# Sample units of an attention kernel: cached keys stored feature by key, their gain moved to the queries

## The chip, the cores and the metric

The kernel runs on one core of a Trainium2 chip, in one launch. The metric is the device time of one execution in microseconds (us).

## The reference

One inference step of a two-layer encoder on a prompt of 1024 tokens and on 8 running streams ("samples") of 16 tokens each, model width 1024, 16 query heads, 4 key/value heads, head width 64. Layer A attends over a window of its own chunk and two before, with a penalty on distance and a learned sink; layer B over its own chunk and eight before, with a learned bias. Both end in a squared-ReLU MLP. What matters here is the attention of the samples, over 128 cached positions and the 16 new ones:

```
k = rmsnorm(k, g_k); q = rmsnorm(q, g_q)          # new tokens
k_all = concatenate([cache_k, k], axis=1)          # 128 cached + 16 new
s = einsum('bqhgd,bkhd->bhgqk', q, k_all) * 64**-0.5 + bias
p = softmax(s)                                     # with a sink in layer A
o = einsum('bhgqk,bkhd->bqhgd', p, v_all)
```

The cached keys come normed and with g_k in them; g_q and the factor 1/8 belong to the queries.

## The kernel before

Tokens stand in nine tiles of 128: eight of the prompt and one, called ST, that holds the 8 x 16 sample tokens. Each layer has an attention stage (0 to about 425 us and 1110 to 1640 us of the trace) and an MLP stage (the rest). All products run on TensorE in fp32r, where a value is kept as a high and a low part (`split`, L127: ScalarE writes the high part, VectorE or GpSimd the difference), so that a projection takes three products per block.

In the attention stage a loop over 16 steps takes two groups (a prompt tile and a key/value head) per step through scores, softmax, transposes of the probabilities (`ps_tr`, L326) and the product with the values (`ps_pv`, L333 and L334). Projections of queries, keys and output (L219 to L221, L176 to L178) are woven in between. Beside them step s carries sample unit U(s): key/value head j = s // 4 and a pair bp = s % 4 of sample streams. A unit is a generator of five pieces that the loop inserts into two steps:

- piece 0 loads the cached keys `kc` and values `vc` of the two streams (128 keys by 2 x 64 features), the queries `qu` (high and low part stacked over 128 partitions, and once swapped), and the 32 new keys into the last 32 columns of `kb`; it multiplies `kc` by the gain g_q x (-1/8) (L560, on GpSimd in layer A, on VectorE in layer B, by the letter c of the layer's `eng`), and writes high and low part side by side into `uks` (L570, L571, both GpSimd);
- piece 1 multiplies each stream's `uks` (keys by [high, low]) with the identity on TensorE, which turns it into features by keys, the high part on partitions 0 to 63 and the low part on 64 to 127 (L577, two products per unit, into `ps_utr`), and ScalarE copies that into `kb` (L578);
- piece 2 makes the scores, two products of 288 columns (L582), and the softmax of the unit on VectorE and ScalarE; piece 3 transposes the probabilities (L607 to L609), piece 4 multiplies them with the values (L615 to L617) and stores the result.

`kc`, `uks` and `kb` have one buffer each. The gain stands on the keys everywhere: of the prompt's and of the new sample keys in `k_stack` (L302), where the new sample keys take only g_q (kout is given), since they have been multiplied by g_k for the output (L295). Queries are normed without a gain in `q_stage1` (L224 to L242), transposed in `q_stage2`, and those of ST go through DRAM to the units.

What the order of instructions is: the program text gives dependences and priorities, and the framework's scheduler then orders each engine's queue by a model of its own. An edit in one piece therefore moves rows on every engine in the same stage.

Of the kernel before, what the change touches and what calls it, by code (L numbers as in the profile page):

```python
# [8 lines left out]
F32 = mybir.dt.float32  # L9
F32R = mybir.dt.float32r  # L10
AF = mybir.ActivationFunctionType
ALU = mybir.AluOpType
# [4 lines left out]
P = 128  # L17
# [3 lines left out]
ST = NT  # L21
NTILE = NT + 1
H = 16
KV = 4
G = 4
HD = 64
# [68 lines left out]
class Build:  # L95
# [127 lines left out]
    def q_stage1(self, work, small, ps, t, nb, fold):  # L223
        nc = self.nc  # L224
        ps3 = ps.rearrange("p (h d) -> p h d", d=HD)
        qn = self.scratch([P, 8, HD], F32, "qn")
        qr = work.tile([P, 8, HD], F32, tag="qr", name="qr", bufs=self.qrb)
        nc.scalar.activation(qn, ps3, AF.Square)
        nc.scalar.copy(qr, ps3)
        ssq = small.tile([P, 8], F32, tag="qssq", name="qssq")  # L230
        nc.vector.tensor_reduce(ssq, qn, AX.X, ALU.add)
        ms = small.tile([P, 8], F32, tag="qms", name="qms")
        e = self.ex[:, t : t + 1]
        if fold:
            c = C_SL2 + nb * 8
            nc.vector.scalar_tensor_tensor(ms, ssq, e, self.cst[:, c : c + 8], ALU.add, ALU.mult)
        else:
            nc.vector.tensor_scalar(ms, ssq, e, 1.0 / HD, ALU.add, ALU.mult)
        rs = small.tile([P, 8], F32, tag="qrs", name="qrs")
        nc.gpsimd.tensor_tensor(rs, ms, self.mhalf[:, 0:8], ALU.pow)  # L240
        self.eng("q").tensor_tensor(qr, qr, rs.unsqueeze(2).to_broadcast([P, 8, HD]), ALU.mult)
        return qr  # L242

    def q_stage2(self, qpool, qr, t):
# [25 lines left out]
    def kv_stage1(self, work, small, ps, t, gk, gq8, gkq8, vst, v8, kout, vout):  # L270
        nc = self.nc
        ps3 = ps[:, 0:256].rearrange("p (h d) -> p h d", d=HD)
        kw = work.tile([P, 2, KV, HD], F32, tag="kw", name="kw")
        kr, kn = kw[:, 0], kw[:, 1]
        r = self.rx[:, t : t + 1]
        if vst is not None:
            pv3 = ps[:, 256:512].rearrange("p (h d) -> p h d", d=HD)
            nc.scalar.activation(vst[:, :, 0:HD], pv3, AF.Copy, scale=r)
            nc.vector.scalar_tensor_tensor(
                vst[:, :, HD:P], pv3, r, vst[:, :, 0:HD].bitcast(F32), ALU.mult, ALU.subtract  # L280
            )
        if vout is not None:
            vsb = v8 if v8 is not None else self.scratch([P, 256], F32, "vsb")
            nc.scalar.activation(vsb, ps[:, 256:512], AF.Copy, scale=r)
        nc.scalar.copy(kr, ps3)
        nc.scalar.activation(kn, ps3, AF.Square)
        ssq = small.tile([P, KV], F32, tag="kssq", name="kssq")
        nc.vector.tensor_reduce(ssq, kn, AX.X, ALU.add)
        ms = small.tile([P, KV], F32, tag="kms", name="kms")
        nc.vector.tensor_scalar(ms, ssq, self.ex[:, t : t + 1], 1.0 / HD, ALU.add, ALU.mult)  # L290
        rs = small.tile([P, KV], F32, tag="krs", name="krs")
        nc.gpsimd.tensor_tensor(rs, ms, self.mhalf[:, 0:KV], ALU.pow)
        nc.vector.tensor_tensor(kn, kr, rs.unsqueeze(2).to_broadcast([P, KV, HD]), ALU.mult)
        if kout is not None:
            nc.vector.tensor_tensor(kn, kn, gk.unsqueeze(1).to_broadcast([P, KV, HD]), ALU.mult)  # L295
            nc.sync.dma_start(kout, kn.rearrange("p h d -> p (h d)"))
        if vout is not None:
            nc.sync.dma_start(vout, vsb)
        return self.k_stack(work, kn, gq8 if kout is not None else gkq8)

    def k_stack(self, work, kn, gq8):
        nc = self.nc  # L302
        ks = work.tile([P, KV, HD], F32, tag="ks", name="ks")
        nc.vector.tensor_tensor(ks, kn, gq8.unsqueeze(1).to_broadcast([P, KV, HD]), ALU.mult)
        return ks

    def k_transpose(self, ks, dst):
# [228 lines left out]
                self.qT8d[layer][2 * nb + j], qTs[j].rearrange("p h q -> p (h q)").bitcast(F32)  # L536
            )

    def unit(self, up, small, layer, bp, j, v8, gq8, cache_k, cache_v):
        nc = self.nc  # L540
        kc = up.tile([P, 2, HD], F32, tag="kc", name="kc")
        nc.sync.dma_start(kc, cache_k[2 * bp : 2 * bp + 2, :, j, :].rearrange("b k d -> k b d"))
        vc = up.tile([P, 2, HD], F32, tag="vc", name="vc")
        nc.sync.dma_start(vc, cache_v[2 * bp : 2 * bp + 2, :, j, :].rearrange("b k d -> k b d"))
        qu = up.tile([P, 2, P], F32R, tag="qu", name="qu")
# [4 lines left out]
        kb = up.tile([P, 288], F32R, tag="kb", name="kb")  # L550
# [5 lines left out]
        else:  # L556
            bias = up.tile([P, 288], F32, tag="ub", name="ub")
            nc.sync.dma_start(bias, self.biasSd[j])
        kp = kc
        self.eng("c").tensor_tensor(kp, kc, gq8.unsqueeze(1).to_broadcast([P, 2, HD]), ALU.mult)  # L560
        if "p" in self.engs:
            yield
            a, b = slice(0, 64), slice(64, 128)
            pt = self.psum("u", [P, P], "ps_utr")
            nc.tensor.transpose(pt, kp.rearrange("p b d -> p (b d)"), self.ident)
            self.split(kb[a, 0:P], kb[b, 0:P], pt[a])
            self.split(kb[b, P : 2 * P], kb[a, P : 2 * P], pt[b])
        else:
            ks = up.tile([P, 2, P], F32R, tag="uks", name="uks")
            nc.gpsimd.tensor_copy(ks[:, :, 0:HD], kp)  # L570
            self.eng("u").tensor_tensor(  # L571
                ks[:, :, HD:P], kp, ks[:, :, 0:HD].bitcast(F32), ALU.subtract
            )
            yield
            pt = self.psum("u", [P, 2, P], "ps_utr")
            for b in range(2):
                nc.tensor.matmul(pt[:, b, :], ks[:, b, :], self.identr, start=True, stop=True)  # L577
            nc.scalar.copy(kb[:, 0:256], pt.rearrange("p b k -> p (b k)"))  # L578
        yield
        s = self.psum("u", [P, 288], "ps_us")  # L580
        for v in range(2):
# [4 lines left out]
        p = up.tile([P, 288], F32, tag="sp", name="sp") if layer == 0 else bias  # L586
# [782 lines left out]
    def attention(self, layer):  # L1369
        nc, I = self.nc, self.ins  # L1370
        A = layer == 0
        if A:
            wkv_src, kv0, gkv = I["w_qkv_a"][0], 1024, 0
            wq_src, gq = I["w_qkv_a"][0], 0
            wo_src = I["w_o_a"][0]
            g_k, g_q = I["g_k_a"][0], I["g_q_a"][0]
            ck, cv = I["cache_k_a"][0], I["cache_v_a"][0]
        else:
            wkv_src, kv0, gkv = I["w_kv"], 0, 4
            wq_src, gq = I["w_q_b"][0], 1  # L1380
            wo_src = I["w_o_b"][0]
            g_k, g_q = I["g_k_b"], I["g_q_b"][0]
            ck, cv = I["cache_k_b"], I["cache_v_b"]
        cfg = CFG[layer]
        psp = () if A else cfg["psp"]
        self.engs = cfg["eng"]
# [1 line left out]
        with ExitStack() as st:  # L1388
# [187 lines left out]

            def U(n):
                j, bp = n // 4, n % 4
                return self.unit(up, small, layer, bp, j, v8, gq8, ck, cv)

            def addend():
                self.last = self.scratch([P, 4, P], F32, "o2")
# [80 lines left out]
                if not cfg["late"]:  # L1663
                    N(ST, "p")
            gk = self.load_gvec(ring, g_k, "gk")
            gq8 = self.load_gvec(ring, g_q, "gq", -0.125)
            gkq8 = ring.tile([P, HD], F32, tag="gkq", name="gkq")
            nc.vector.tensor_tensor(gkq8, gk, gq8, ALU.mult)
            if A:
# [107 lines left out]
            for s in range(2 * NT):  # L1777
                u = U(s)
# [133 lines left out]
```

## Time and profile before

| | |
|---|---|
| median of 3 runs | 2356.03 us |
| the three runs | 2350.42, 2356.03, 2356.86 us |
| span of the profiled execution | 2349.6 us |
| time of the profiled execution outside its span | not recorded; its span lies 0.8 us under the fastest run |
| TensorE matmuls | busy 2273.2 us, 97% of the span |
| TensorE weight loads | busy 1899.3 us, 81% |
| VectorE, ScalarE, GpSimd | 73%, 57%, 27% |
| idle TensorE by the page | 2349.6 - 2273.2 = 76.4 us |

PE is TensorE's matmuls, PEld its weight loads, DVE VectorE, ACT ScalarE, POOL GpSimd, SP SyncE, which issues most transfers. A matmul's recorded duration overlaps those of its neighbours, since they are pipelined; what one occupies is read from the distance between starts. A wait names the line that waited and the line whose end released it. L12 is line 12 of the kernel before.

### The profile page before, as it was taken

The page shows a single profiled execution, that of the slowest core. Times are in us where ns is not written, and L with a number is a line of the kernel's source. Part 1 is how long each engine was busy: PE and PEld are TensorE (multiplying, and loading weights), DVE is VectorE, ACT ScalarE, POOL GpSimd, SP SyncE. Part 2 cuts the span into 40 slices and gives each one's busy share as a digit, 9 for nine tenths or more (in the row PEclk, how much of TensorE's full clock was granted, in tenths as well). Part 3 has the DMA queues.
Part 4 walks back from the last instruction along what each step waited for, and adds up shares of the span by engine and source line. Part 5 has one row for each costly group of instructions (what it writes and reads, how often), then busy time and mean ns, then how long its engine had stood idle before and what let it go on. Part 6 is the DMA issues. An engine that isn't in the chain of part 4 may idle for free.

```text
span 2349.6 us, 33397 instructions
## 1 busy us (share of the span) xinstructions
PE 2273.2 (97%) x11429; PEld 1899.3 (81%) x11429; DVE 1718.3 (73%) x3075; ACT 1332.0 (57%) x2684; POOL 644.7 (27%) x950
## 2 busy tenths in 40 slices
PE   8999999899999999999899899999899999999999
PEld 6787877788888888778778778887888888888887
DVE  6888786766656578898577776877666566678987
ACT  3777674555555555344377666665655555555443
POOL 4434332313213111002433444345132132210011
PEclk9999999999999999999999999999999999999999
DMA  7435546234334687848654656555243343877567
GB/s 262 128 103 177 166 141 208 89 122 162 132 112 152 218 231 174 272 142 206 191 157 114 190 151 180 166 172 186 72 162 132 114 160 113 276 212 197 183 165 198
DMA packets 226715, 392.70 MB, mean 167 GB/s; under 512 B 51592, under 2 KB 126288, under 8 KB 226448
## 3 DMA queue, kind: packets, MB, share of 16 engines
q1 hardware_dynamic: 188816, 283.58, 37.8%
q0 software_dynamic: 36432, 102.26, 16.0%
q10 hardware_dynamic: 1296, 4.72, 0.5%
q8 instruction: 90, 1.47, 0.3%
q14 instruction: 81, 0.66, 0.1%
HBM read 236.51 MB, written 156.85 MB: 167 GB/s over the span
## 4 chain that ended last, share of the span: by engine, by line
PE 73%; DVE 11%; DMA 8%; ACT 3%; issue 2%; POOL 2%; SPq 1%; ACTq 0%; DVEq 0%; POOLq 0%
PE ps_c L745 7%; PE ps_c L746 7%; PE ps_c L747 7%; PE ps_x L745 5%; PE ps_x L747 5%; PE ps_x L746 5%; PE ps_mm L219 3%; PE ps_mm L221 3%; PE ps_mm L220 3%; PE ps_y L747 2%; PE ps_y L746 2%; PE ps_y L745 2%; PE ps_tr L326 2%; DMA a<-hd 2%; DVE w L134 1%
## 5 line engine op out<-in xcount | busy, mean ns | idle before, releaser
L746 PE MATMUL ps_c<-w,a 128*128 128x512 f32 x960 | 374.0, 390 | 3.9 <-DVE w L134 3.9
L745 PE MATMUL ps_c<-w,a 128*128 128x512 f32 x960 | 374.1, 390 | 3.2 <-ACT o L1165 1.7
L747 PE MATMUL ps_c<-w,a 128*128 128x512 f32 x960 | 373.5, 389 | 0.0
L910 POOL DMA_DIRECT2D hd<-h x272 | 149.4, 552 | 594.3 <-ACT h L819 378.4
L745 PEld LDWEIGHTS ps_c<-w,a 128*128 128x128 f32 x960 | 180.2, 188 | 42.9 <-issue 2.7
L746 PEld LDWEIGHTS ps_c<-w,a 128*128 128x128 f32 x960 | 180.2, 188 | 42.7 <-DVE w L134 5.6
L747 PEld LDWEIGHTS ps_c<-w,a 128*128 128x128 f32 x960 | 180.2, 188 | 37.4
L128 ACT CAST a<-a 128x1536 fp32r<-128x1536 f32 x80 | 118.6, 1483 | 154.6 <-DMA a<-hd 154.6
L219 PE MATMUL ps_mm<-w,hh 128*128 128x512 f32 x432 | 173.9, 403 | 12.8 <-ACT hh L128 5.4
L221 PE MATMUL ps_mm<-w,hl 128*128 128x512 f32 x432 | 172.4, 399 | 1.4 <-DVE hl L134 1.2
L220 PE MATMUL ps_mm<-w,hh 128*128 128x512 f32 x432 | 171.4, 397 | 0.3
L134 DVE TENSOR_TENSOR a<-a 128x1536 fp32r<-128x1536 f32 x80 | 140.6, 1757 | 40.6 <-ACT a L128 40.5
L745 PE MATMUL ps_x<-sx,w 128*128 128x512 f32 (+1 forms) x408 | 157.8, 387 | 4.5 <-ACT h L866 2.7
L128 ACT CAST w<-ru 128x512 fp32r<-128x512 f32 (+1 forms) x160 | 109.9, 708 | 84.4 <-PE ps_y L746 32.0
L128 ACT CAST w<-s 128x2048 fp32r<-128x2048 f32 x56 | 107.1, 1912 | 88.2 <-DVE s L1062 78.8
L747 PE MATMUL ps_x<-sx,w 128*128 128x512 f32 (+1 forms) x408 | 154.2, 378 | 0.3 <-DVE w L134 0.3
L746 PE MATMUL ps_x<-sx,w 128*128 128x512 f32 (+1 forms) x408 | 154.1, 378 | 0.0
L134 DVE TENSOR_TENSOR w<-s,w 128x2048 fp32r<-128x2048 f32 x56 | 128.2, 2289 | 32.3 <-ACT w L128 32.0
L1182 POOL DMA_DIRECT2D xp<-o x28 | 36.2, 1294 | 411.6 <-ACT o L1165 391.0
L134 DVE TENSOR_TENSOR w<-ru,w 128x512 fp32r<-128x512 f32 (+1 forms) x160 | 129.7, 813 | 14.8 <-ACT w L128 14.7
L134 DVE TENSOR_TENSOR ptl<-ps_tr,pth 128x512 fp32r<-128x512 f32 x180 | 122.5, 685 | 21.2 <-ACT pth L128 17.5
L818 ACT ACTIVATE h<-h 128x512 f32<-128x512 f32 (+1 forms) x102 | 61.9, 607 | 122.1 <-DVE h L868 93.0
(274 smaller groups left out, 6152.9 us busy)
## 6 DMA issues: line engine op xcount, KB each, us to landing
a<-hd SPq DMA_DIRECT2D x80, 768.0 KB, 6.2
hd<-h POOLq DMA_DIRECT2D x272, 192.0 KB, 2.5
ru<-in_w_up SPq DMA_DIRECT2D x64, 512.0 KB, 3.9
r<-in_w_down SPq DMA_DIRECT2D x32, 1024.0 KB, 9.8
xp<-o POOLq DMA_DIRECT2D x28, 768.0 KB, 9.5
o<-oTd SPq DMA_DIRECT2D x50, 256.0 KB, 3.9
x<-xp SPq DMA_DIRECT2D x23, 512.0 KB, 5.5
xp<-xo SPq DMA_DIRECT2D x18, 512.0 KB, 2.9
```

What stands on the lines that cost most here:

```text
L128: a = nc.scalar.copy(hi, src)
L134: return a, e.tensor_tensor(lo, src, hi.bitcast(F32), ALU.subtract)
L219: nc.tensor.matmul(ps, a, w[:, 0, k, :], start=(k == 0), stop=False)
L220: nc.tensor.matmul(ps, a, w[:, 1, k, :], start=False, stop=False)
L221: self.lp = nc.tensor.matmul(ps, b, w[:, 0, k, :], start=False, stop=(k == KC - 1))
L326: self.lp = nc.tensor.transpose(pt[:, i, :], get(i), self.ident)
L745: a = mm(ps, ah, bh, start=first, stop=False, skip_group_check=True)
L746: mm(ps, ah, bl, start=False, stop=False, skip_group_check=True)
L747: return a, mm(ps, al, bh, start=False, stop=last, skip_group_check=True)
L818: a = nc.scalar.activation(t, src, AF.Relu)
L910: return lambda p, z: self.nc.gpsimd.dma_start(self.hd[c // 4][:, p, c % 4], z)
L1182: nc.gpsimd.dma_start(dst, z, accum_op=ALU.add)
```

## The change

The host lays the cached keys out once more, as an input of its own: for each head and pair of streams a block of 128 rows by 256 columns, whose rows 0 to 63 are the features and whose columns are the keys of both streams; rows 64 to 127 repeat them. A unit loads that block with one transfer, ScalarE rounds all 128 rows into `kb` (high part), and GpSimd replaces the lower 64 rows by the difference (low part). L560, L570, L571, the two products L577 and the copy L578 go, and with them `uks` and `ps_utr`. The gain g_q x (-1/8) now multiplies the normed queries of tile ST (one VectorE instruction per half and layer), so the new sample keys go without it: `k_stack` is folded into `kv_stage1`, which returns the keys of ST unscaled, in the buffer `kw`.

```diff
@@ q_stage1
         self.eng("q").tensor_tensor(qr, qr, rs.unsqueeze(2).to_broadcast([P, 8, HD]), ALU.mult)
+        if t == ST:
+            nc.vector.tensor_tensor(
+                qr, qr, self.gq8.unsqueeze(1).to_broadcast([P, 8, HD]), ALU.mult
+            )
         return qr
@@ kv_stage1
-        return self.k_stack(work, kn, gq8 if kout is not None else gkq8)
-
-    def k_stack(self, work, kn, gq8):
-        nc = self.nc
+        if t == ST:
+            return kn
         ks = work.tile([P, KV, HD], F32, tag="ks", name="ks")
-        nc.vector.tensor_tensor(ks, kn, gq8.unsqueeze(1).to_broadcast([P, KV, HD]), ALU.mult)
+        g = gq8 if kout is not None else gkq8
+        nc.vector.tensor_tensor(ks, kn, g.unsqueeze(1).to_broadcast([P, KV, HD]), ALU.mult)
         return ks
@@ unit
-        kc = up.tile([P, 2, HD], F32, tag="kc", name="kc")
-        nc.sync.dma_start(kc, cache_k[2 * bp : 2 * bp + 2, :, j, :].rearrange("b k d -> k b d"))
+        kc = up.tile([P, 2 * P], F32, tag="kc", name="kc")
+        nc.sync.dma_start(kc, cache_k[j, bp])
...
-        kp = kc
-        self.eng("c").tensor_tensor(kp, kc, gq8.unsqueeze(1).to_broadcast([P, 2, HD]), ALU.mult)
-        if "p" in self.engs:
...
-        else:
-            ks = up.tile([P, 2, P], F32R, tag="uks", name="uks")
-            nc.gpsimd.tensor_copy(ks[:, :, 0:HD], kp)
-            self.eng("u").tensor_tensor(
-                ks[:, :, HD:P], kp, ks[:, :, 0:HD].bitcast(F32), ALU.subtract
-            )
-            yield
-            pt = self.psum("u", [P, 2, P], "ps_utr")
-            for b in range(2):
-                nc.tensor.matmul(pt[:, b, :], ks[:, b, :], self.identr, start=True, stop=True)
-            nc.scalar.copy(kb[:, 0:256], pt.rearrange("p b k -> p (b k)"))
+        yield
+        cached, low = kb[:, 0 : 2 * P], slice(64, 128)
+        nc.scalar.copy(cached, kc)
+        self.eng("u").tensor_tensor(
+            cached[low], kc[low], cached[low].bitcast(F32), ALU.subtract
+        )
         yield
         s = self.psum("u", [P, 288], "ps_us")
@@ kernel
+    for n, a in (("k_t_a", inputs["cache_k_a"][0]), ("k_t_b", inputs["cache_k_b"])):
+        a = np.asarray(a).reshape(4, 2, P, KV, HD).transpose(3, 0, 4, 1, 2)
+        given[n] = np.ascontiguousarray(np.concatenate([a, a], 2).reshape(KV, 4, P, 2 * P))
```

Three places of the order of instructions, since the scheduler moves rows that the diff does not show. In the changed kernel's rows the line numbers are its own: L326 has become L329, L333 and L334 have become L336 and L337, L382 has become L385, L262 has become L266, L582 has become L571, L405 has become L408, L607 to L609 have become L596 to L598.

TensorE, layer A, unit 7, from the transposes of one group's probabilities to the unit's scores. Before:

```order
L326 MATMUL ps_tr<-identr,p 128x128 x4
L333 MATMUL ps_pv<-pth,VS 128x512
L334 MATMUL ps_pv<-ptl,VS 128x512
L577 MATMUL ps_utr<-identr,uks 128x128 x2
L176 MATMUL ps_mm<-w,oh 128x512
...
L178 MATMUL ps_mm<-w,ol 128x512
L326 MATMUL ps_tr<-identr,p 128x128 x4
L382 MATMUL ps_s<-KT,qT 128x256 x4
L582 MATMUL ps_us<-kb,qu 128x288 x2
```

And of the change:

```order
L329 MATMUL ps_tr<-identr,p 128x128 x4
L337 MATMUL ps_pv<-ptl,VS 128x512
L329 MATMUL ps_tr<-identr,p 128x128 x4
L176 MATMUL ps_mm<-w,oh 128x512
...
L178 MATMUL ps_mm<-w,ol 128x512
L385 MATMUL ps_s<-KT,qT 128x256 x4
L571 MATMUL ps_us<-kb,qu 128x288 x2
```

The two products L577 are gone, the twelve output projections in the middle stay, and the second set of transposes has moved ahead of them.

GpSimd, layer A, units 9 and 10: `p` is a group's probabilities, which L405 (now L408) divides by their sums before TensorE transposes them; `pn` and `qrs` are a zeroed tile and the norms of queries. Before:

```order
L570 CAST uks_3351<-kc_3340 128x2x64
L571 TENSOR_TENSOR uks_3351<-kc_3340,uks_3351 128x2x64
L560 TENSOR_TENSOR kc_3584<-kc_3584,gq_311 128x128
L405 TENSOR_SCALAR p_3266<-p_3266,li_3386 128x128 x4
L585 MEMSET pn_3527 128x128
L240 TENSOR_TENSOR qrs_3445<-qms_3443,mhalf_68 128x8
L570 CAST uks_3595<-kc_3584 128x2x64
L405 TENSOR_SCALAR p_3395<-p_3395,li_3492 128x256 x4
L571 TENSOR_TENSOR uks_3595<-kc_3584,uks_3595 128x2x64
```

And of the change:

```order
L574 MEMSET pn_3467 128x128
L240 TENSOR_TENSOR qrs_3387<-qms_3385,mhalf_68 128x8
L408 TENSOR_SCALAR p_3337<-p_3337,li_3434 128x256 x4
L565 TENSOR_TENSOR kb_3532<-kc_3524,kb_3532 64x256
L408 TENSOR_SCALAR p_3443<-p_3443,li_3567 128x256 x4
L574 MEMSET pn_3726 128x128
L240 TENSOR_TENSOR qrs_3638<-qms_3636,mhalf_68 128x8
L565 TENSOR_TENSOR kb_3793<-kc_3785,kb_3793 64x256
L408 TENSOR_SCALAR p_3598<-p_3598,li_3684 128x256 x4
```

Three GpSimd instructions of a unit have become one, which still stands ahead of a group of `p`.

TensorE, layer A, from the transposes of a prompt tile's queries (`ps_q` from `qr`) to the first scores that read the tile `qT` made of them. Before (where rows are left out lie 26, of which 25 are single products of 512 columns and one is four transposes):

```order
L262 MATMUL ps_q_1311<-identr_66,qr_1174 128x128 x4
L382 MATMUL ps_s_1368<-KT_207,qT_1014 128x256 x2
L333 MATMUL ps_pv_1302<-pth_1266,VS_208 128x512
...
L382 MATMUL ps_s_1415<-KT_207,qT_1316 128x256
```

And of the change, with all rows:

```order
L266 MATMUL ps_q_1298<-identr_66,qr_1163 128x128 x4
L329 MATMUL ps_tr_1342<-identr_66,p_1102 128x128 x4
L336 MATMUL ps_pv_1289<-pth_1253,VS_208 128x512
L385 MATMUL ps_s_1351<-KT_207,qT_1007 128x256 x3
L337 MATMUL ps_pv_1289<-ptl_1254,VS_208 128x512
L596 MATMUL ps_utp_1379<-identr_66,sp_1233 128x128
L597 MATMUL ps_utp_1379<-identr_66,sp_1233 128x128
L598 MATMUL ps_utp_1379<-identr_66,pn_1231 128x128
L329 MATMUL ps_tr_1385<-identr_66,p_1102 128x128 x4
L385 MATMUL ps_s_1398<-KT_207,qT_1303 128x256
```

The first score of the new `qT` has moved up to follow its transposes closely.

## Rows read from the trace of the kernel before

**Rows 1.** The page: span, busy time of each engine, and TensorE's granted clock in tenths.

```profile
span 2349.6 us, 33397 instructions
...
PE 2273.2 (97%) x11429; PEld 1899.3 (81%) x11429; DVE 1718.3 (73%) x3075; ACT 1332.0 (57%) x2684; POOL 644.7 (27%) x950
...
PEclk9999999999999999999999999999999999999999
```

**Rows 2.** Windows by stage: length, busy us of PE, PEld, DVE, ACT, POOL, clock, transfers.

```profile
0.00:425.00 425.00, 400.71 (x2137) 330.74 (x2138) 328.68 (x960) 272.16 (x751) 167.93 (x271) 1.00 0.52 169
425.00:1110.00 685.00, 671.97 (x3237) 564.20 (x3236) 492.73 (x544) 362.72 (x526) 126.06 (x189) 1.00 0.56 167
1110.00:1640.00 530.00, 504.40 (x2710) 419.49 (x2709) 390.82 (x1018) 326.78 (x874) 220.58 (x289) 0.99 0.56 170
1640.00:2349.00 709.00, 696.15 (x3352) 584.83 (x3350) 506.02 (x555) 370.38 (x536) 130.15 (x202) 1.00 0.54 164
```

**Rows 3.** Waits of PE, 75 to 425 us: in total, times, longest.

```profile
PE ps_pv L333 <- ACT pth L128: 2.1, 1, 2.1
PE ps_tr L326 <- POOL p L405: 1.6, 2, 0.9
```

**Rows 4.** Waits of PE, 1110 to 1640 us.

```profile
PE ps_pv L334 <- DVE ptl L134: 2.7, 6, 1.5
PE ps_sn L433 <- DVE qT L134: 2.2, 1, 2.2
...
PE ps_tr L326 <- POOL p L483: 0.6, 1, 0.6
```

**Rows 5.** Instructions of the tile ps_utr: count, duration min/median/max.

```profile
L577 PEld LDWEIGHTS ps_utr<-identr,uks x64: 187/190/245, 74.7 to 1606.1; 128*128 128x128 f32 x64
L577 PE MATMUL ps_utr<-identr,uks x64: 218/276/309, 74.7 to 1606.2; 128*128 128x128 f32 x64
```

**Rows 6.** Timeline of weight loads about one pair (start us, us), layer A, after transposes.

```profile
273.67 0.42 PEld L326 LDWEIGHTS ps_tr<-identr,p 128*128 128x128 f32 x4 [0.17 <-issue]
274.06 0.30 PEld L577 LDWEIGHTS ps_utr<-identr,uks 128*128 128x128 f32 x2
274.28 0.19 PEld L334 LDWEIGHTS ps_pv<-ptl,VS 128*128 128x128 f32 x1
```

**Rows 7.** The same about a pair between products of 512 columns.

```profile
328.12 0.19 PEld L334 LDWEIGHTS ps_pv<-ptl,VS 128*128 128x128 f32 x1
328.35 0.42 PEld L577 LDWEIGHTS ps_utr<-identr,uks 128*128 128x128 f32 x2
328.69 0.19 PEld L178 LDWEIGHTS ps_mm<-w,ol 128*128 128x128 f32 x1
328.80 0.19 PEld L176 LDWEIGHTS ps_mm<-w,oh 128*128 128x128 f32 x1
329.04 0.19 PEld L177 LDWEIGHTS ps_mm<-w,oh 128*128 128x128 f32 x1
```

**Rows 8.** Groups of POOL by form: busy us, mean ns, idle before and releaser.

```profile
L405 POOL TENSOR_SCALAR p<-p,li 128x256 f32<-128x256 f32 x112 | 53.8, 501 | 63.6 <-DVE li L418 51.3 <-ACT qT L128 5.3 <-DVE nm L392 4.7
L343 POOL TENSOR_TENSOR o<-o,o 128x512 f32<-128x512 f32 x14 | 18.0, 1286 | 35.7 <-DMA o<-oTd 35.6
L571 POOL TENSOR_TENSOR uks<-kc,uks 128x128 fp32r<-128x128 f32 x32 | 16.6, 519 | 1.7
L570 POOL CAST uks<-kc 128x128 fp32r<-128x128 f32 x32 | 10.7, 335 | 33.6 <-PE ps_utr L577 30.7 <-DVE kc L560 2.8
L560 POOL TENSOR_TENSOR kc<-kc,gq 128x128 f32<-128x128 f32 x16 | 8.5, 530 | 32.0 <-DMA kc<-in_cache_k_a 32.0
```

**Rows 9.** Groups of ACT by form.

```profile
L128 ACT CAST w<-ru 128x512 fp32r<-128x512 f32 x128 | 76.4, 621 | 47.9 <-DVE ru L808 23.6 <-DVE ru L805 21.9 <-DVE ru L807 2.4
L128 ACT CAST qT<-ps_q 64x512 fp32r<-64x512 f32 x64 | 37.2, 582 | 14.2 <-DVE qT L134 8.9 <-PE ps_q L262 4.6
L578 ACT CAST kb<-ps_utr 128x256 fp32r<-128x256 f32 x32 | 12.2, 381 | 3.3 <-PE ps_utr L577 3.0
```

**Rows 10.** Groups of DVE by form.

```profile
L134 DVE TENSOR_TENSOR qT<-ps_q,qT 64x512 fp32r<-64x512 f32 x64 | 44.1, 689 | 5.7 <-ACT qT L128 3.8
L241 DVE TENSOR_TENSOR qr<-qr,qrs 128x512 f32<-128x512 f32 x36 | 25.6, 711 | 4.4 <-POOL qrs L240 4.2
L560 DVE TENSOR_TENSOR kc<-kc,gq 128x128 f32<-128x128 f32 x16 | 6.8, 423 | 11.7 <-DMA kc<-in_cache_k_b 11.5
L304 DVE TENSOR_TENSOR ks<-kw,gq 128x256 f32<-128x256 f32 x7 | 3.3, 465 | 0.1
```

More of the change, by code (lines that the diff above doesn't have):

```diff
@@ L537, in spill_sample, with unit @@
             )
-    def unit(self, up, small, layer, bp, j, v8, gq8, cache_k, cache_v):
+    def unit(self, up, small, layer, bp, j, v8, cache_k, cache_v):
         nc = self.nc
-        kc = up.tile([P, 2, HD], F32, tag="kc", name="kc")
-        nc.sync.dma_start(kc, cache_k[2 * bp : 2 * bp + 2, :, j, :].rearrange("b k d -> k b d"))
+        kc = up.tile([P, 2 * P], F32, tag="kc", name="kc")
+        nc.sync.dma_start(kc, cache_k[j, bp])
         vc = up.tile([P, 2, HD], F32, tag="vc", name="vc")
@@ L558, in unit @@
             nc.sync.dma_start(bias, self.biasSd[j])
-        kp = kc
-        self.eng("c").tensor_tensor(kp, kc, gq8.unsqueeze(1).to_broadcast([P, 2, HD]), ALU.mult)
-        if "p" in self.engs:
-            yield
[L563 to L567, printed above, removed]
-        else:
-            ks = up.tile([P, 2, P], F32R, tag="uks", name="uks")
-            nc.gpsimd.tensor_copy(ks[:, :, 0:HD], kp)
-            self.eng("u").tensor_tensor(
-                ks[:, :, HD:P], kp, ks[:, :, 0:HD].bitcast(F32), ALU.subtract
-            )
-            yield
-            pt = self.psum("u", [P, 2, P], "ps_utr")
-            for b in range(2):
-                nc.tensor.matmul(pt[:, b, :], ks[:, b, :], self.identr, start=True, stop=True)
-            nc.scalar.copy(kb[:, 0:256], pt.rearrange("p b k -> p (b k)"))
+        yield
[4 more added lines that the diff above has]
+        )
         yield
@@ L1376, in attention @@
             g_k, g_q = I["g_k_a"][0], I["g_q_a"][0]
-            ck, cv = I["cache_k_a"][0], I["cache_v_a"][0]
+            ck, cv = I["k_t_a"], I["cache_v_a"][0]
         else:
@@ L1382, in attention @@
             g_k, g_q = I["g_k_b"], I["g_q_b"][0]
-            ck, cv = I["cache_k_b"], I["cache_v_b"]
+            ck, cv = I["k_t_b"], I["cache_v_b"]
         cfg = CFG[layer]
@@ L1578, in U @@
                 j, bp = n // 4, n % 4
-                return self.unit(up, small, layer, bp, j, v8, gq8, ck, cv)
+                return self.unit(up, small, layer, bp, j, v8, ck, cv)
             def addend():
@@ L1665, in attention @@
             gk = self.load_gvec(ring, g_k, "gk")
-            gq8 = self.load_gvec(ring, g_q, "gq", -0.125)
+            self.gq8 = gq8 = self.load_gvec(ring, g_q, "gq", -0.125)
             gkq8 = ring.tile([P, HD], F32, tag="gkq", name="gkq")
```

## The prediction

> **What bounds the kernel now.** I read the page first. TensorE's matmuls are busy 97% of the span, at a granted clock of nine tenths or more in every slice, and no other engine comes above 73% [rows 1]. So the span is what TensorE's stream of instructions occupies, plus 2349.6 - 2273.2 = 76.4 us in which it stands idle. The windows by stage show where the change can act: the attention stages hold 425 - 400.7 = 24.3 us and 530 - 504.4 = 25.6 us of that idle time, the MLP stages the rest [rows 2], and TensorE's order of instructions in the MLP stages is the same in the changed kernel. Then the waits of PE inside the attention stages: they are many and short, the longest of a kind some 2 us, and none names the sample units' keys [rows 3, 4]. Two things can therefore move the time: what TensorE no longer has to do, and how well the new order covers its waits.
>
> **What leaves TensorE.** 32 units lose two products each, 64 in all. One lasts 0.276 us in the median and its weight load 0.190 us [rows 5], but they overlap their neighbours, so I take the distance between starts. After transposes, the pair's loads begin at 274.06 and the next load at 274.28: 0.22 us for two [rows 6]. Between products of 512 columns, the load of L334 starts at 328.12 and that of L176 at 328.80, with L334's product and the pair between them: 0.68 us. Two steps of the 512-column stream are 0.46 us (328.12 to 328.35, 328.80 to 329.04), which leaves 0.22 us for the pair [rows 7]. So 32 x 0.22 = 7.0 us; some pairs show a little more, and I take 0.225, which makes 7.2 us. Bounds: the four transposes ahead of the pair start within 0.39 us, 0.098 each [rows 6], which would make 64 x 0.098 = 6.3 us; the largest distance from a pair's first load to the next engine row, 0.34 us [rows 7], would make 10.9 us, but holds the end of the product before. All of this lies on the path, since TensorE is what everything else waits for.
>
> The Trainium skill speaks against a part of that: "TensorE: Matmul & The Clock Gate", section "Back-to-back issue gap", gives about 81 ns per product for a sustained stream of loads and products with 128 columns, where the trace shows about 110. By it the 64 products would be worth 64 x 0.081 = 5.2 us, and the sum would stop at 2350.8 us, an estimate from that page. The trace's own distance decides here.
>
> **ScalarE.** 32 copies of 128x256 out of PSUM, 0.381 us each, become 32 copies of the same size out of SBUF. The nearest SBUF copy is 128x512 with 0.621 us [rows 9], so one costs between 0.38 and 0.62; half the columns puts it near 0.40. That is between 0 and 7.7 us over the kernel, near 1 us, on an engine that is 57% busy: hidden, unless a copy delays a softmax behind it, which a rival below prices.
>
> **GpSimd.** A unit loses L570 and L571 (0.335 + 0.519), in layer A L560 too (0.530) [rows 8], and gains one difference of 64x256. Bounds are 0.519, if only the number of elements counts (64x256 is as many as 128x128), and 1.286, the 128x512 sum of L343 [rows 8]. I take the middle by columns, about 0.78. That is 1.38 to 0.78 us per unit in layer A and 0.85 to 0.78 in layer B: no load added. GpSimd is 27% busy; before a group's probabilities it mostly stands idle for VectorE's sums, 51.3 us on L405 alone [rows 8].
>
> **VectorE.** L560 goes in layer B (16 x 0.423 = 6.8 us), and so do the two products for ST's keys (2 x 0.465); four products of 128x512 come (0.711 by L241, 2.8 us) [rows 10]. Net -4.9 us on a 73% busy engine. TensorE waits for VectorE in layer B for `ptl` and `qT`, 2.7 and 2.2 us [rows 4], so some of it may come back; I count nothing. On the queries of ST the added 0.711 us stands between norm and transposes. That chain has two groups of other work to hide behind; without the cover it is 4 x 0.711 = 2.8 us at most.
>
> **Transfers and queues.** As many transfers as before, on the same queue; each `kc` brings twice the bytes in rows of 1 KB instead of pieces of 256 bytes. Nothing of TensorE waits for it now. What waits for it changes: L560 stood idle 32.0 us in layer A and 11.5 us in layer B for that load [rows 8, 10], on engines with room. In the changed order ScalarE waits for it, then GpSimd for ScalarE, and both queues are in order: behind the difference on GpSimd stands a group of `p`, behind the copy on ScalarE stand exponentials. The cover is time: the load is issued in piece 0, the copy belongs to piece 1, half a step later. On `kb` the score products now wait for GpSimd. In the order, the transposes of the group of `p` that follows the difference on GpSimd come ahead of the unit's scores on TensorE in 28 of 32 units, so there the difference has long ended; in four units of layer B it is closer.
>
> **The new order.** Counting TensorE's work between rows (0.23 us per 512 columns, 0.11 per 128 [rows 6, 7]), I compared the room between a result and its reader. From scores to the transposes of their probabilities the smallest room in layer A goes from 4.4 to 5.2 us, from these transposes to the first product with `ptl` it is 1.2 us in four places before and in one now: looser. From the queries' transposes to the first reader of `qT` it is tighter: under 5 us in 4 places before, in 12 now; in the place shown, 2.1 us (11 rows of 128 columns, 3 of 256, 2 of 512) against 6.7. One ScalarE copy and one VectorE difference, 0.582 + 0.689 = 1.3 us [rows 9, 10], have to fit in. I let these cancel.
>
> **Sum.** -7.2 us on TensorE, nothing else on the path: 2349.6 - 7.2 = 2342.4 us of span. The span lies 6.4 us under the median of the runs shown; on the median it makes 2356.0 - 7.2 = 2348.8 us. A measurement of this kernel can tell about 0.3%, 7.1 us, from no change: the forecast lies on that very edge.
>
> **Rivals.**
> 1. *The tighter `qT` places eat the gain.* Eight new places with little room; the longest wait of that kind now is 2.2 us [rows 4]. At 0.8 us each 6.4 us come back: 2355 us, no change. For it: ScalarE and VectorE have queues of other work in these places. Against: 1.3 us is less than 2.1. Chance 0.24.
> 2. *The looser places pay too.* Waits for `ptl` and `pth` of 2.7 and 2.1 us [rows 3, 4] shrink, VectorE has 4.9 us less to do: 3 to 4 us more, 2345 us. Chance 0.14.
> 3. *Slower: the load of the keys reaches ScalarE.* If the copy into `kb` is queued too soon after its load, it stands on ScalarE as L560 did, up to 43.5 us in all (32.0 + 11.5), with exponentials behind it and `p` behind the difference. The change turns into no gain when 7.2 of these reach TensorE, and into a loss that can be measured from 14.3 us, a third of the total. At half, 21.8 us, the time is 2356.0 - 7.2 + 21.8 = 2371 us; at 40%, 2366. For it: both queues are strict in the order shown. Against: half a step of cover, and TensorE waits for `p` only 1.6 and 0.6 us now [rows 3, 4]. Chance 0.09.
> 4. *A product on identity holds TensorE for all of its recorded 0.276 us* [rows 5]: 64 x 0.276 = 17.7 us, 2338 us. Against it stand the 0.22 us of [rows 6]. The Trainium skill, "TensorE: Matmul & The Clock Gate", section "Part 4: PE-mode transpose", gives about 275 ns for a transpose in a kernel's context, which agrees with the duration, not with the distance. Chance 0.03.
> 5. *A product is worth less than the distance shows*, as transposes in a row do (0.098 us, 6.3 us, 2349.8 us) or less: no change, at 2350 to 2351. The Trainium skill's 81 ns per product are of this kind. Chance 0.06.
>
> That the products do not leave can be ruled out: TensorE's order has 64 rows fewer.
>
> **How the numbers follow.** The forecast, 2348.8 us with 3 us to either side for waits that shift, has 0.44; half of it falls below 2349.0, the edge for faster. Faster: 0.22 + 0.14 + 0.03 = 0.39, raised to 0.41 because the three runs shown spread over 6.4 us and a low draw counts as faster. Same: 0.22 + 0.24 + 0.06 = 0.52, less 0.02. Slower: 0.09, of which a part would end within 0.3%: 0.09 with the tail of rival 1. The range goes from 2342 (rival 2 with its spread) to 2358 (rival 1 with its spread), which leaves out most of rivals 3 and 4 and the tails, near 0.17.
>
> **What would show it.** Right: TensorE with 64 products fewer, the MLP stages as long as before within 1 us, the attention stages together about 7 us shorter, idle time in them still near 50 us. The copy into `kb` about 0.40 us without idle time for its load, the difference about 0.8 us. Wrong: waits of PE for `qT` of more than 5 us in all (rival 1), idle time of ScalarE for `kc` (rival 3), or attention stages shorter by 15 us (rival 4).

## The result, and the profile after

The changed kernel takes 2365.31 us (median of 13 runs, 2359.46 to 2370.62), the kernel before 2356.03: ratio 1.0037, 95% interval 1.0026 to 1.0049. It is slower by 0.37%, 9.3 us, where 2348.8 was forecast. The profiled execution took 2361.56 us. Page of the changed kernel, against [rows 1]:

```profile
span 2359.6 us, 33253 instructions
...
PE 2276.4 (96%) x11365; PEld 1899.6 (81%) x11365; DVE 1711.8 (73%) x3061; ACT 1331.0 (56%) x2684; POOL 635.8 (27%) x902
...
PEclk9998999999999999999999999999999999999999
```

The 64 products are gone (11429 to 11365), and yet TensorE is busy 3.2 us longer. The windows by stage (columns as in [rows 2], with exact borders: attention A, MLP A, attention B, MLP B), changed kernel:

```profile
0.00:432.80 432.80, 404.01 (x2116) 333.08 (x2116) 330.28 (x963) 272.66 (x753) 160.20 (x240) 0.98 0.51 168
432.80:1141.10 708.30, 695.51 (x3327) 583.95 (x3325) 507.89 (x555) 367.59 (x531) 133.14 (x198) 0.99 0.56 168
1141.10:1652.00 510.90, 481.04 (x2589) 397.47 (x2587) 370.95 (x994) 322.69 (x871) 216.37 (x266) 0.99 0.55 170
1652.00:2359.60 707.60, 695.86 (x3340) 585.09 (x3340) 502.69 (x552) 368.12 (x531) 126.07 (x200) 0.99 0.54 165
```

and the two attention stages of the kernel before, cut at the same marks:

```profile
0.00:426.10 426.10, 401.81 (x2147) 331.72 (x2148) 329.78 (x961) 273.26 (x753) 168.56 (x272) 1.00 0.52 168
...
1132.40:1640.60 508.20, 482.60 (x2617) 401.54 (x2615) 375.88 (x1005) 320.34 (x867) 211.26 (x280) 0.99 0.55 168
```

The attention stages grew by 6.7 and 2.7 us where 7 us less were forecast. Their idle time went from 24.3 + 25.6 = 49.9 to 28.8 + 29.9 = 58.7 us, and the granted clock of the first stage from 1.00 to 0.98. The new instructions themselves are as forecast, 0.41 and near 0.8 us (groups by form; the difference's median is 0.737 us):

```profile
L564 ACT CAST kb<-kc 128x256 fp32r<-128x256 f32 x32 | 13.1, 411 | 6.6 <-PE ps_us L571 4.2 <-POOL p L486 1.3 <-DMA kc<-in_k_t_b 0.6
L565 POOL TENSOR_TENSOR kb<-kc,kb 64x256 fp32r<-64x256 f32 x32 | 26.7, 833 | 48.1 <-ACT kb L564 23.5 <-issue 19.4 <-DMA oTd<-so 2.8
```

Waits of PE in attention B of the changed kernel (in total, times, longest), against [rows 4]:

```profile
PE ps_mm L219 <- ACT hh L128: 4.1, 1, 4.1
PE ps_n L212 <- ACT x L1154: 3.3, 2, 2.5
PE ps_pv L337 <- DVE ptl L134: 2.9, 7, 0.8
PE ps_sf L436 <- ACT p L473: 2.8, 5, 1.0
PE ps_mm L219 <- DMA hh<-hTd: 2.5, 2, 1.7
PE ps_n L681 <- DVE sx L134: 2.4, 2, 1.2
PE ps_sn L436 <- DVE qT L134: 2.2, 1, 2.2
PE ps_x L734 <- ACT sx L128: 1.6, 1, 1.6
```

`qT` waits as before. Longer than in the kernel before are the waits for `x` (0.7 us there) and for the `p` that scores wait for (1.0 there); shorter are those for `hh`, at the stage's start (5.4 and 4.0 there). The waits for `sx` lie about the stage's end: from 1100 to 1700 us products of L681 (before: L692) wait 5.5 us for it in the changed kernel and 5.4 in the kernel before.

### The profile page after: what moved, and what is told of

The parts are those of the page before. It is cut to its first block, busy times and chain, and to the rows that moved or that the text cites. A ratio compares the mean times of both kernels' runs of the same rounds, so it can differ in the third digit from the quotient of the medians.

```text
span 2359.6 us, 33253 instructions
## 1 busy us (share of the span) xinstructions
PE 2276.4 (96%) x11365; PEld 1899.6 (81%) x11365; DVE 1711.8 (73%) x3061; ACT 1331.0 (56%) x2684; POOL 635.8 (27%) x902
## 4 chain that ended last, share of the span: by engine, by line
PE 80%; DVE 8%; DMA 7%; ACT 2%; issue 2%; POOL 1%; SPq 0%; ACTq 0%; DVEq 0%; POOLq 0%
PE ps_c L734 8%; PE ps_c L735 8%; PE ps_c L736 8%; PE ps_x L734 5%; PE ps_x L735 5%; PE ps_x L736 5%; PE ps_mm L219 4%; PE ps_mm L221 4%; PE ps_mm L220 4%; PE ps_y L736 2%; PE ps_y L734 2%; PE ps_y L735 2%; PE ps_tr L329 2%; DMA a<-hd 2%; PE ps_mm L176 2%
```

## The experiments

Three theories at the start. **A:** the scheduler's new order of all queues costs more than the products give. **B:** the new path of a unit costs it. **C:** TensorE, with less to do, is granted less clock. To hold an order, each engine's instructions that two kernels share are chained with dependencies that fix the order of issue and wait for nothing (`PINNED` holds, for each engine, the places of the instructions to be chained):

```
+    for e, (n, order) in json.loads(zlib.decompress(base64.b85decode(PINNED))).items():
+        z = made[e]
...
+        for d in order:
+            at += d
+            rows.append(z[at])
+        for a, b in zip(rows, rows[1:]):
+            tc.add_manual_dep(b, a.name, AFTER, reason="order")
```

All results (ratio to the kernel before with its 95% interval; the clock is the mean over a kernel's runs):

| run | what it is | median us | ratio | clock |
|---|---|---|---|---|
| after_again | changed kernel, once more | 2366.31 | 1.0040 (1.0024 to 1.0056) | 0.988 |
| a_in_b | changed, old order | 2349.03 | 0.9965 (0.9954 to 0.9977) | 0.9926 |
| b_in_a | before, new order | 2379.49 | 1.0102 (1.0084 to 1.0119) | 0.989 |
| pin_pe | changed, old order on TensorE alone | 2356.20 | 0.9994 (0.9980 to 1.0009) | 0.990 |
| pin_A | changed, old order in layer A | 2368.52 | 1.0055 (1.0037 to 1.0074) | 0.9885 |
| pin_B | changed, old order in layer B | 2347.87 | 0.9961 (0.9946 to 0.9976) | 0.992 |
| pin_b1 | changed, old order in B's first half | 2356.51 | 1.0009 (0.9995 to 1.0023) | 0.988 |
| pin_b2 | changed, old order in B's second half | 2359.62 | 1.0027 (1.0011 to 1.0044) | 0.989 |
| pin_tail | changed, old order at B's end | 2363.62 | 1.0034 (1.0019 to 1.0050) | 0.989 |
| prod_back | a_in_b, the 64 products back | 2351.83 | 0.9985 (0.9970 to 1.0000) | 0.992 |
| prod_x4 | a_in_b with 256 products | 2368.31 | 1.0057 (1.0036 to 1.0079) | 0.992 |
| dve_back | a_in_b, 16 scalings on VectorE | 2357.13 | 1.0003 (0.9989 to 1.0016) | 0.992 |
| before_c | before, B's scaling on GpSimd, order held | 2346.14 | 0.9954 (0.9938 to 0.9969) | 0.993 |
| before_c_free | the same, order free | 2343.36 | 0.9945 (0.9926 to 0.9964) | 0.993 |
| fill | a_in_b, two waits filled | 2350.05 | 0.9975 (0.9964 to 0.9987) | 0.993 |
| a_in_bc | changed, order of before_c_free | 2349.56 | 0.9979 (0.9968 to 0.9991) | 0.993 |

The kernel before had medians of 2355.1 to 2355.8 us and mean clocks of 0.992 to 0.993 beside them, and 2354.89 us in its second profiled execution. The runs are not all from one chip, so a difference of a few us between two medians is read from their ratios.

### Order or path?

> The changed kernel's work in the order of the kernel before: every engine's instructions that both kernels have are chained, by order-only dependencies, into the sequence of the kernel before; only the new differences, the gain's products on ST's queries and the loads of the cached keys are placed by the scheduler. Theory A (the new order costs about 9.3 + 7.2 = 16 us, the removed products give back 7): 2349 us, ratio 0.997, and half-clock stretches near the 31 us of the kernel before. Theory B (the new path of a unit, copy, difference, product, or its transfers, costs it): 2362 to 2366 us, ratio above 1.002, as in the changed kernel. Theory C (with 64 products less, TensorE has gaps after which the granted clock falls): 2360 to 2366 us with near 60 us at half clock.

> The other way round: the work of the kernel before in the order of the changed kernel; what only the kernel before has (the scaling, the rounding, the 64 products, the copies into kb) and the loads of the keys are placed by the scheduler. Theory A: 2365 + 7 = 2372 us, ratio near 1.007, half-clock stretches near 60 us. Theories B and C: 2356 us, ratio 1.000, with 31 us at half clock. Between the two, about 2364, if half of the cost is the order's.

> The changed kernel once more, for a second profiled execution and a second ratio. If the places where the granted clock falls belong to the kernel's order (theory A), they lie where they lay (195 to 215, 430 to 455, 1145 to 1160, 1655 to 1680 us, and a few single ones) with 50 to 65 us in all at half clock; if they are chance of one execution, the sum and the places differ by tens of us while the time stays at 2365.

> The kernel before once more, for a second profiled execution: 2356 us; half-clock stretches of 25 to 37 us in all, at 200 to 210, 430 to 440, 1135 to 1150, 1305 to 1340 and 1645 to 1655 us, if they belong to the order; elsewhere and of another sum if they are chance.

A holds from both sides: 17.3 us between the same work in two orders (2366.31 to 2349.03), and the old work loses 24 us in the new order. That is 7 more than A's 16 to 17; TensorE waits 6.0 us for `kb` in layer A there, so the longer old path comes late in the new order, and it was followed no further. B and C fall as causes of these 17 us: path and missing products are in a_in_b too. That the path costs nothing does not follow; what it takes from the gain is met below. Attention A and B of a_in_b:

```profile
0.00:431.80 431.80, 402.49 (x2116) 330.01 (x2116) 331.20 (x963) 274.45 (x754) 158.67 (x240) 0.99 0.52 169
1142.70:1640.20 497.50, 479.21 (x2585) 397.34 (x2583) 372.84 (x988) 318.36 (x864) 209.79 (x264) 0.99 0.57 174
```

Attention B idles 18.3 us against 29.9 in the changed kernel and 30.7 in its second profiled execution. Of the waits listed above, `x` is gone, `ptl` and `p` are halved, `hh` is shorter and `qT` stays (waits of PE in attention B of a_in_b):

```profile
PE ps_mm L219 <- ACT hh L128: 3.0, 1, 3.0
PE ps_sn L436 <- DVE qT L134: 2.2, 1, 2.2
PE ps_pv L337 <- DVE ptl L134: 1.4, 6, 0.5
...
PE ps_sf L436 <- ACT p L473: 1.2, 3, 0.5
```

The second profiled executions repeat the waits within 1 us or so, the places of half clock only in part; in all (summed over windows of 5 us) the kernel before is at half clock for some 31 and 34 us, the changed one for 59 and 65, a_in_b for 48, b_in_a for 65. So a_in_b has the time that A expected, but not the 31 us at half clock.

### Which part of the order?

> The changed kernel with the order of the kernel before in layer A alone; layer B is left to the scheduler. By the stage lengths of the two profiled executions of the changed kernel (attention A 432.8 and 436.8 us, B 510.9 and 514.1) against the run in the old order (431.8 and 497.5), layer A's order costs 1 to 5 us and layer B's 13 to 17: then this run stands at 2361 to 2365 us, ratio near 1.003. Rival: the cost is the granted clock's fall in layer A (17 and 26 us at half clock there): then 2353 us.

> The order of the kernel before in layer B alone, layer A left to the scheduler. If layer B's order makes the loss: 2366 - 15 = 2351 us, ratio 0.998; by the rival (layer A's granted clock) 2362 us. If the two layers' costs don't add, both runs stand above 2355.

> Only TensorE's instructions chained into the order of the kernel before; ScalarE, VectorE, GpSimd and the load queue are ordered by the scheduler round that. If TensorE's own order makes the loss: 2349 to 2351 us, ratio 0.997. If it is the queues of the engines that feed it, which put results late: 2358 us or more.

All of it is layer B's: held there alone, the old order gives the whole 18.4 us, held in layer A nothing (2368.5 us, above the expected 2361 to 2365). So the 6.7 us by which attention A grew are not the order's: it takes 431.8 us in a_in_b too. TensorE's own order gives 10 of the 17, between the two readings on record; the rest comes back when the queues that feed it are held as well.

> The changed kernel with only the last part of layer B (what the program writes after its last product with V: the last output-projection blocks, the norms and their transposes) chained into the order of the kernel before; all the rest is the scheduler's as in the changed kernel. From the last eviction of a product with V to the first product of the MLP, the profiled executions show 34.1 us in the changed kernel's order and 25.3 us in the old order; until there the new order is 4.5 to 8 us behind. If this end makes half of the loss: 2366 - 9 = 2357 us, ratio 1.0005, and 25 to 26 us for that stretch. Rival: the end only shows a delay that was made earlier (results late from the body), and the stretch stays at 32 to 34 us: 2364 to 2366 us.

The rival holds. The end of the layer, from the last copy of a product with V (1617.80 us) to the first product of the MLP (1652.00), takes 34 us in the changed kernel and 25 in the old order, but with the end alone held it still takes 32, and the time falls by 2.7 us only, which is within the noise (1.0034 against 1.0040). TensorE now stands before the output projection there, 2.8 us for `xo`: what comes late was made late.

> The changed kernel with the first half of layer B (up to the 16th group's product with V, as the program writes it) chained into the order of the kernel before; layer A and the second half are the scheduler's. If the first half makes the loss (it is 3.6 us behind in the first 70 us and 7 us behind at the 14th group): 2349 to 2352 us, ratio 0.998. If the second half does (from 4 us behind at the 29th group to 13 at the stage's end): 2361 to 2366 us.

> The second half of layer B, with the projection and the norms at its end, chained into the old order; layer A and the first half of B are the scheduler's. If the second half makes the loss: 2348 to 2352 us, ratio 0.998. If the first: 2361 to 2366 us. If both runs come out between, near 2357, the loss is spread over the layer.

The third reading, spread over the layer: by the medians the first half gives back 9.8 us and the second 6.7; by the ratios 7 and 3, and the 3 are within the noise. Neither half brings the mean clock back (0.988 and 0.989), both together do (0.992). No single wait carries the loss.

The pin runs chain only a part of the instructions: one engine's, or those that the program writes in that layer, half or end.

### What are the products worth?

```
+        pt = self.psum("u", [P, 2, P], "ps_utr")
+        for b in range(2):
+            nc.tensor.matmul(pt[:, b, :], qu[:, b, :], self.identr, start=True, stop=True)
```

> The changed kernel in the order of the kernel before (the run that gave 0.9965), with the 64 products on identity put back at their old places on TensorE. They take the landed queries of the unit as operand and nobody reads their result, so TensorE has all its old work and nothing else of the old path is back. If the products are what the change saves (the prediction's 0.225 us per pair): 2349 + 7.2 = 2356 us, ratio 1.000. If a product is worth nothing, because the gain came from shorter waits: 2349 to 2350 us, ratio 0.9965. At the recorded 0.276 us each: 2367 us.

> As the run with the 64 products put back (0.9985), with four pairs per unit in the place of each pair: 256 products that nobody reads, in the old order. At the prediction's 0.225 us per pair: 2349 + 128 x 0.225 = 2378 us, ratio 1.009. At 0.09 us per pair, as the medians of the single pair gave: 2349 + 11 = 2360 us, ratio 1.002. If only part lies in TensorE's waits, in between, with idle time of the attention stages shorter by the difference.

(prod_x4 goes through the pair four times.) By medians the first pair of a unit costs 2.8 / 32 = 0.09 us, by the ratios 0.0020 x 2355 / 32 = 0.15 with an uncertainty as large; over all four, 0.0092 x 2355 / 128 = 0.17 us. So the 64 products are worth 5.4 us by that slope (4 to 7 by the intervals), not 7.2. TensorE's busy time in the attention stages agrees: 21.5 us more in prod_x4 than in a_in_b, 0.17 per pair. The added products read `qu`, which the old ones did not, and TensorE waits 2.2 us for it in prod_x4; without that wait the slope would make 4.9 us. Attention A of prod_back, against a_in_b's above, shows where the rest is:

```profile
0.00:430.70 430.70, 406.04 (x2147) 334.37 (x2148) 331.86 (x963) 273.86 (x753) 158.95 (x240) 0.98 0.52 169
```

3.5 us more work, and 24.7 us idle instead of 29.3: in this stage TensorE waits for the others in the time that it no longer works. Other executions agree: with the products attention A is idle for 23.8 to 25.4 us (before twice, before_c_free, prod_x4; 27.3 in before_c), without them for 28 to 33 (after twice, dve_back, a_in_bc and the pin runs; 26.2 in fill, where a wait of that stage is filled).

### Where does the old order's gain come from?

In a_in_b attention B is 10.7 us shorter than before; the products don't explain that.

> The kernel before in its own order, with one thing moved: the scaling of the cached keys in layer B goes from VectorE to GpSimd, as layer A has it. In the old order the changed path makes attention B 498 us long against 507 before, though the 32 products put back cost only 1.6 us of it. If what is saved there is VectorE's 16 scalings, with their 11.5 us of waiting for the load of the keys ahead of work that TensorE needs: attention B near 500 us and 2350 us in all, ratio 0.997. If it is the shorter chain to kb (no product, no PSUM buffer held for it): 2355 to 2357 us, ratio 1.000.

> The reverse: the changed kernel in the old order, and on VectorE, in the places of the old scalings of layer B, 16 products of 128x128 of the landed keys with the gain into a tile that nobody reads (the keys get a second buffer in layer B, so that this reader holds up no load). If VectorE's scalings and their waits for the load were the cost: attention B back to 503 to 506 us, 2355 us, ratio 0.999 to 1.000. If not: 498 us and 2349 us.

before_c is one letter in the settings of layer B, dve_back one product in piece 0 and a second buffer for the keys:

```
-... eng='Ogu', ...
+... eng='Ocgu', ...
```

```
-        kc = up.tile([P, 2 * P], F32, tag="kc", name="kc")
+        kc = up.tile([P, 2 * P], F32, tag="kc", name="kc", bufs=1 + layer)
...
+        if layer == 1:
+            again = up.tile([P, 2, HD], F32, tag="again", name="kc")
+            nc.vector.tensor_tensor(
+                again, kc[:, 0:P].rearrange("p (b d) -> p b d", b=2),
+                self.gq8.unsqueeze(1).to_broadcast([P, 2, HD]), ALU.mult,
+            )
```

before_c gives 0.46%, 10.8 us (9.7 by the medians), with all 64 products in place, and in dve_back 16 scalings put back on VectorE take 9 us away from a_in_b. Attention B of before_c, then of dve_back:

```profile
1141.20:1637.40 496.20, 480.63 (x2616) 401.07 (x2615) 370.00 (x987) 319.21 (x865) 217.06 (x296) 0.99 0.56 172
```

```profile
1139.30:1643.20 503.90, 476.64 (x2585) 393.39 (x2584) 376.29 (x1004) 318.61 (x864) 208.74 (x263) 1.00 0.55 171
```

Idle time 15.6 against 27.3 us. In dve_back VectorE's 16 products of 0.29 us (median) stand idle for the keys' load (instructions of the tile `kc` there, and what their engine sat idle for):

```profile
L564 DVE TENSOR_TENSOR kc<-kc,gq x16: 280/291/1225, 1154.3 to 1548.2; 128x128 f32<-128x128 f32 x16
...
  DMA kc<-in_k_t_b: 15.2, 9
```

That is the wait of 11.5 us in [rows 10]. TensorE needs what VectorE would have done meanwhile: these are its waits for `ptl` and `qr` in attention B of dve_back, where a_in_b has 1.4 us for `ptl` at L337, 0.3 at L266 and none for `qr`:

```profile
PE ps_pv L337 <- DVE ptl L134: 2.7, 7, 1.3
...
PE ps_q L266 <- DVE qr L241: 2.2, 1, 2.2
PE ps_q L266 <- DVE ptl L134: 2.0, 2, 1.7
```

How much of the cost is the wait for the load and how much the 16 x 0.29 = 4.7 us of work on VectorE was not tried apart. On GpSimd the same wait is longer, 16.9 us in before_c, and costs nothing that shows.

> The kernel before with the scaling of layer B's cached keys on GpSimd and nothing held: the scheduler orders it as it likes. With the old order held this gave 2346 us (0.9954). If the gain is VectorE's: 2344 to 2350 us. If the scheduler's new order decides, as it did in the changed kernel: anything between 2346 and 2365; its order differs in 396 of TensorE's 11271 rows from the kernel before, where the changed kernel differs in 6150, so I expect under 2350.

The gain survives the scheduler's own order: this is the fastest kernel of the study, faster than both.

### The granted clock

> The changed kernel in the old order (0.9965), with products that nobody reads put into two of TensorE's waits: 7 of 512 columns ahead of the product that waits 2.1 us for hl near 25 us, 10 ahead of the first product of attention B, which waits 3 us for hh. If the granted clock falls because of these waits, the stretches at half clock at 25 to 35 us (3.4 us) and 1145 to 1155 us (7 to 10 us) are gone, which gives back half of their length, 5 us: 2344 us, ratio 0.994. If the falls have another cause they stay, and the time is 2349 us; if the added products push back what follows, 2350 to 2351 us.

```
+    def fill(self, ps, w, n):
+        for _ in range(n):
+            self.nc.tensor.matmul(ps, self.identr, w[:, 0, 0, :], start=True, stop=True)
```

Near 25 us of a_in_b (timeline of PE: start, duration, idle before):

```profile
24.30 0.39 PE L221 MATMUL ps_mm<-w,hl 128*128 128x512 f32 x1
24.52 0.39 PE L219 MATMUL ps_mm<-w,hh 128*128 128x512 f32 x1
...
27.25 0.67 PE L221 MATMUL ps_mm<-w,hl 128*128 128x512 f32 x1 [2.11 <-DVE hl L134]
27.72 0.63 PE L219 MATMUL ps_mm<-w,hh 128*128 128x512 f32 x1
28.15 0.63 PE L220 MATMUL ps_mm<-w,hh 128*128 128x512 f32 x1
```

After the wait the products start 0.43 us apart instead of 0.23: half of the 2.4 GHz. The windows of 25 to 30 us, a_in_b and then fill:

```profile
25.00:30.00 5.00, 2.89 (x8) 2.19 (x8) 3.56 (x5) 0.26 (x1) 1.76 (x3) 0.74 1.02 377
```

```profile
25.00:30.00 5.00, 4.38 (x20) 3.24 (x19) 4.07 (x6) 0.21 (x1) 1.85 (x3) 1.00 1.05 401
```

With the wait filled but for 0.62 us the clock stays; at the start of attention B the fall was halved, with 2.9 us of waiting left. That is one execution, and it does not show that the wait brings on the fall. In the other 18 profiled executions TensorE's order is the same up to this place, and ten of them fall here, after waits of 1.9 to 2.6 us. Eight do not: six after waits of 0.5 to 1.7 us, and two after 2.48 (pin_B) and 2.74 us, the longest of all, in a_in_bc:

```profile
27.10 0.50 PE L221 MATMUL ps_mm<-w,hl 128*128 128x512 f32 x1 [2.74 <-DVE hl L134]
```

```profile
25.00:30.00 5.00, 2.90 (x13) 2.38 (x14) 4.04 (x6) 0.00 (x0) 1.62 (x3) 1.00 1.05 405
```

So falls go with longer waits here, but the length of the wait alone does not decide. In fill the time didn't follow either, 2350 us, and the mean clock over its runs is a_in_b's. A single fall is no term by itself.

### A version from both

> The changed kernel's work, chained into the order that the scheduler gave the kernel before with its layer B scaling on GpSimd (0.9945, 2343.4 us). Both have VectorE free of that scaling, so what is left of the change is the 64 products: if they are worth 0.09 to 0.17 us a pair there too, 2343 - 3 to 5 = 2338 to 2341 us, ratio 0.993. If the products lie in waits in this order, 2343 us.

A miss: 0.9979, worse than before_c_free's 0.9945. Attention A of before_c_free, then of a_in_bc:

```profile
0.00:428.20 428.20, 404.45 (x2146) 333.12 (x2147) 331.02 (x961) 273.06 (x753) 167.08 (x272) 0.99 0.52 168
```

```profile
0.00:427.80 427.80, 399.42 (x2116) 328.30 (x2116) 331.29 (x963) 274.67 (x754) 160.13 (x240) 0.99 0.52 170
```

5.0 us less work, 4.6 us more idle time. The changed unit gains nothing there that moving the scaling had not given. That is not the whole difference: by the ratios a_in_bc is 8 us slower, while the spans of these two executions are 0.5 us apart (2344.1 and 2344.6). What of its path (the copy on ScalarE, the difference on GpSimd, twice the bytes) costs that, or whether it is an order that was made for other work, was not tried apart.

## Why the prediction was wrong, step by step

- **"The new order: I let these cancel"** is the step that failed. The order costs 17 us, so the forecast would have been near right without it: 2349.03 us in the old order. The rooms I counted were the wrong measure: for `qT`, where they became tighter, TensorE waits 3.0 us in all, 3.2 before. The loss is many short waits in attention B, 29.9 us of idle time against 18.3 in the old order: `x` 3.3 us against none, `ptl` 2.9 against 1.4, `p` 2.8 against 1.2, `hh` 4.1 against 3.0, and others. Why the scheduler's new order of the feeding queues makes these results late was not followed to single instructions.
- **No term for the granted clock.** Every kernel that has half or more of layer B in the new order runs at 0.988 to 0.989, those with B in the old order at 0.992 to 0.993, and pin_pe between them. Over single runs, time against clock falls by 1700 us per unit in 118 runs of the kernel before and by 1500 in 21 of the changed one (correlation -0.66 and -0.85), so 0.0044 of clock goes with 7 us. If TensorE had work all that time it would be 0.0044 x 2360 = 10 us. But to go with the clock is not to be caused by it, and other figures give the clock less. The two profiled executions of the changed kernel have spans 12.6 and 21.1 us longer than a_in_b's; 12.4 and 15.7 of that are idle time and only 0.2 and 5.4 longer busy time, where a slower clock would show. pin_b1 gave back 7 to 10 us at an unchanged 0.988. So most of the loss is waiting, and the clock's share stays open. That the new order's waits bring on the falls is not shown.
- **"-7.2 us on TensorE"** was mis-sized: 5.4 us by prod_x4's slope, 2.8 by prod_back's median. The distance between starts counts also what fits into waits nearby, as the idle time of attention A showed. (Its two steps from [rows 7] make 0.47 us, not 0.46, which moves the price by 0.3 us only.) Rival 5, a product worth less than the distance shows, had the size. The 81 ns per product of the Trainium skill, "TensorE: Matmul & The Clock Gate", section "Back-to-back issue gap", would make 5.2 us, an estimate from that page; the slope of 0.085 us per product agrees.
- **VectorE, "I count nothing"**: the largest gain of all, 9 to 11 us, lay in the 16 scalings of layer B, with the wait of 11.5 us that [rows 10] showed. The prediction read that wait as one "on engines with room"; by before_c and dve_back VectorE, 73% busy, had none there. Rival 2 had the direction at 3 to 4 us.
- So it is luck that the sum came out in the old order, -6.5 us (-8 by the ratio) against -7.2: 9 to 11 + 5 us of gains, less some 6 to 10 us that are left over. That these came back through the new path is a remainder and not a measurement; a_in_bc, 8 us behind before_c_free, agrees with it.
- **ScalarE and GpSimd** were right: 0.407 and 0.737 us in the median against 0.40 and 0.78. Rival 3, the only one that ended slower, is false: ScalarE waited for the load once, 0.6 us. Rival 1 put a loss in the order, but at `qT`, and its sign, more than 5 us of waiting there, is absent. So no rival named the mechanism that made the kernel slower.
- **"MLP stages as long as before within 1 us"**: 708.3 and 707.6 against 706.3 and 709.0, but two executions of the kernel before differ by 7 us in the first of them (706.3 and 713.0), so the test was too sharp.

## What to carry to other kernels

Where a scheduler orders the queues, an edit is two changes, the work and the order: hold the old order with order-only dependencies to measure the first alone, before believing either. A busy engine that stands in its own queue for a load is a place to look first, even when another engine is the bound: here a letter that moves 16 small instructions to an engine that is 27% busy is worth more (9 to 11 us) than 64 products of the bounding one (5). Work taken from the bounding engine can come back as its waiting where the engines that feed it are as tight, as in attention A here.

## What the runs showed of the hardware

- Near 25 us a wait of 2.11 us is followed by 3.5 us of products at half clock (a_in_b), one of 1.21 us in the kernel before, at the same place of the same order, by none: its products start 0.23 us apart there. But waits of 2.48 and 2.74 us (pin_B, a_in_bc) are followed by none either. What sets the length of the wait, and what else decides on the fall, was not followed.
- Time and clock move together from run to run of one kernel, 1500 to 1700 us per unit over all runs (1250 to 2510 in single series).
- On GpSimd a difference of 64x256 takes 0.737 us in the median, one of 128x128, with as many elements, 0.465 (L571 of the kernel before): the number of elements alone does not set the time.
